# Biases of two adaLN gates placed in zeroed accumulators before the multiply-adds, and another background rate in the SwiGLU units

## The chip, the core and the metric

The kernel runs on one core of one Trainium2 chip (trn2). The metric is the device time of one execution in microseconds (us). Before the change three runs gave a median of 1597.8 us (1597.12 to 1598.16). Next to them stands one profiled execution with its trace; it took 1597.22 us, of which the profile's span covers 1595.4 us.

## What is computed

One layer of a decoder trunk for 256 tokens of width 2048, all in float32. Cut to what matters here:

```
mod = silu(c) @ w_ada + b_ada                      # 1 x 12288
shift1, scale1, gate1, shift2, scale2, gate2 = split(mod, 6)
h = rms_norm(x) * (1 + scale1) + shift1
x = x + gate1 * mixing_sublayer(h)                 # attention, dilated attention, GLA, w_out
h = rms_norm(x) * (1 + scale2) + shift2
x = x + gate2 * (silu(h @ w_gate) * (h @ w_up)) @ w_ffn_out
```

gate1 and gate2 are rows of 2048 numbers which multiply the columns of the outputs of the two halves. Each is one row vector times a 2048 x 2048 part of w_ada (16.8 MB), plus 2048 numbers of b_ada.

## The kernel before

**Main work.** All large products run on TensorE, in three matmuls for each pair of tiles: weights and activations are split into a high and a low part (`mm3`, lines 164 to 166). Weights come by SyncE's DMA queue (SP) in pieces of 128 x 1024 floats, 512 KB each, into four `raw` buffers (line 146, in the last stages line 1269). ScalarE casts a piece into `whi` (lines 158, 1276), VectorE subtracts to get `wlo` (lines 159, 1277), and there are four buffers of each. A piece feeds twelve matmuls of 512 columns in an ordinary block.

**Order.** The program is written for a tile framework. It works out the order of each engine's instructions ahead of time from priorities and readiness, and puts in the waits. Every engine, and the DMA queue of SP, then works strictly in that order. Loads are written inside `prio()`, which moves them 4000 places forward; a load then stands in the queue as soon as the framework believes that its buffer is free. `tc.issue_after(x)` keeps an instruction behind `x` on its engine.

**Background.** Four of the six parts of `mod` are worked out beside the main work. `ada_segment_steps` yields once for each of 32 loads of w_ada (128 rows x 1024 columns, line 375, into a ring of three or four buffers AR, KC, KD, OD). When the ring is full, `mac` puts the oldest piece's multiply-add on VectorE, behind the last weight split: acc += raw * silu(c) per row (`ada_mac`, line 288). The first piece of each half is a plain product which starts the accumulator (line 286). After the last multiply-add `done` is put into the list `after`. For the gates this is `rows_of`: four small loads of b_ada into a `scr` buffer (line 970) and four additions on row 0 of the accumulator (line 971), then four empty steps, and then for each of four quarters of 512 columns, twice: a cast on ScalarE (line 980), a subtraction on VectorE (line 981), and after two steps two matmuls with a matrix of ones (lines 985, 986), which sum over the 128 rows and spread the result. The quarter goes back to SBUF on ScalarE (line 987). That is 28 steps.

**Rate.** `tick(n)` adds n to a balance and does one step of the background list and one of `after` for each whole one in it. `block` ticks once for each two slices of 128 rows, with `state["rate"]`: RATE_MID 0.6 while gate1 is made, RATE_FFN 0.65 in the eleven units of the SwiGLU's first product, RATE_OUT 2.5 in the last product, where `fast_products` ticks with twice the rate, 5, for each entry of its order.

**Places.** gate1 uses the tiles T4 and T5. Their last readers before it are the matmuls of the GLA levels (lines 800 and 832). gate2 uses the tile `ada`, whose reader before it is the turning of the second normalised input (line 1192), early in unit 0. gate2's background is appended in unit 8; units 8, 9 and 10 are ordinary ones with two blocks of eight ticks each, so 48 ticks in all. Units 1 to 7 save an eighth of their products in the way of Strassen and have no background. After unit 10 comes `fast_products` with the order OUT_A: seven ordinary entries, then the fast ones in turn with ordinary ones. It calls `sums_of_unit` (lines 1432 to 1437, work for VectorE) at entries 1, 2 and 4, and `flush` at entry 7. gate2 is read behind that (line 1417).

Of the kernel before, what the change touches and what calls it, by code (L numbers as in the profile page):

```python
# [17 lines left out]
P = 128  # L18
T = 256
NT = T // P  # L20
D = 2048
KC = D // P
DFF = 5632
NB = 512
# [5 lines left out]
N_DIL = 6  # L30
N_GLA = 4
SEG_SHIFT1, SEG_SCALE1, SEG_GATE1, SEG_SHIFT2, SEG_SCALE2, SEG_GATE2 = range(6)
RATE_IN, RATE_MID, RATE_FFN = 0.8, 0.6, 0.65
RATE_OUT = 2.5
LOOK = 3
DEFER = 4
# [40 lines left out]
def trunk(ctx: ExitStack, tc: tile.TileContext, I, out):  # L77
    nc = tc.nc
# [10 lines left out]
    def nm(base):  # L89
        uid[0] += 1  # L90
        return f"{base}_{uid[0]}"

    def S(tag, shape, dtype=F32):
        return slot.tile(shape, dtype, tag=tag, name=nm(tag))
# [4 lines left out]
    def scr(shape, dtype=F32):  # L99
        return sp.tile(shape, dtype, tag="scr", name=nm("scr"))  # L100
# [4 lines left out]
    def misc_bank(shape):  # L105
        return psm.tile(shape, F32, tag="misc", name=nm("misc"))

    @contextmanager
    def prio(offset=AHEAD):

        with tc.high_priority(offset=offset):
            start = tc.cur_priority
            yield
            n = tc.cur_priority - start
        tc.cur_priority += n
# [164 lines left out]

    w_ada = I["w_ada"]

    def ada_mac(acc, raw, k):
        c = csil[:, k : k + 1]
        if k == 0:
            nc.vector.tensor_scalar(acc, raw, c, None, op0=ALU.mult)
        else:
            nc.vector.scalar_tensor_tensor(acc, raw, c, acc, op0=ALU.mult, op1=ALU.add)  # L288
# [5 lines left out]
    def ada_group(k0, k1, tags=ADA_TAGS, between=None):  # L294
# [5 lines left out]
        for i in range(pieces):  # L300
            a = k0 + n * i // pieces
            m = k0 + n * (i + 1) // pieces - a
            w = m * P
            acc = S("ada", [P, 2, w])
            for k in range(KC):
                with prio():
                    raw = S(tags[count % len(tags)], [P, 2, w])
                    nc.sync.dma_start(
                        raw,
                        w_ada[k * P : (k + 1) * P, : 2 * D].rearrange("p (s c) -> p s c", s=2)[:, :, a * P : a * P + w],  # L310
                    )
                    with tc.issue_after(state["macs_after"]) if "macs_after" in state else nullcontext():
                        ada_mac(acc, raw, k)
                count += 1
                if k < KC - 1:
                    yield
            if between is not None:
                between()
            with prio():
                c = slice(a - k0, a - k0 + m)  # L320
                sums = small([P, 2, m])
                for j in range(2):
                    turned_sums(sums[:, j, :], acc[:, j, :])
                finish_columns(sums[:, 0, :], sh[:, c], SEG_SHIFT1, a)
                finish_columns(sums[:, 1, :], sc[:, c], SEG_SCALE1, a, ROW_N1)
            yield
# [25 lines left out]
    def araw(shape, dtype=F32):  # L352
        ring["n"] += 1
        return S(ring["tags"][ring["n"] % len(ring["tags"])], shape, dtype)

    macs = []

    def mac():
        acc, j, k, raw, done = macs.pop(0)
        with tc.issue_after(state["split"].ins):  # L360
            ada_mac(acc[j], raw, k)
        if done is not None:
            after.append(done)

    def ada_segment_steps(acc, seg, done):


        for k in range(KC):
            for j in range(2):
                while len(macs) >= len(ring["tags"]):  # L370
                    mac()
                raw = araw([P, 2 * NB])
                c0 = seg * D + j * 2 * NB
                with prio():
                    nc.sync.dma_start(raw, w_ada[k * P : (k + 1) * P, c0 : c0 + 2 * NB])
                macs.append((acc, j, k, raw, done if (k, j) == (KC - 1, 1) else None))
                yield

    def last_macs():
        while macs:  # L380
            mac()
            yield
# [121 lines left out]
    def first_group():  # L504
# [28 lines left out]
        for k in range(KC - 1):  # L533
            with tc.issue_after(split.ins) if k > 3 else nullcontext():
                ada_mac(acc, raws[k], k)
# [42 lines left out]
    for g in range(len(GROUPS) - 1):  # L578
        nxt = ada_group(*GROUPS[g + 1])
        steps = KC * -(-(GROUPS[g + 1][1] - GROUPS[g + 1][0]) // 4)  # L580
        done = 0
# [373 lines left out]
    def columns(seg, acc):  # L955
        for _ in range(4):
            yield
        v = const.tile([P, KC], F32, name=nm("mod2"))
        for i in range(0, KC, 4):
            turned_sums(v[:, i : i + 4], acc[:, i * P : (i + 4) * P], state["mm"].ins)  # L960
            yield
        finish_columns(v, v, seg, 0, ROW_N2 if seg == SEG_SCALE2 else None)
        mod2[seg] = v

    def rows_of(name, seg, acc):

        quarters = [a[:, c : c + NB] for a in acc for c in (0, NB)]
        for j, q in enumerate(quarters):
            br = scr([1, NB])
            nc.sync.dma_start(br, I["b_ada"][:, seg * D + j * NB : seg * D + (j + 1) * NB])  # L970
            nc.vector.tensor_add(q[0:1, :], q[0:1, :], br)
            yield
        for _ in range(4):
            yield
        for q in quarters:
            ps = misc_bank([P, NB])
            for c in (slice(0, T), slice(T, NB)):
                hl = S("T6", [P, 2, T], F32R)
                hi, lo = hl[:, 0, :], hl[:, 1, :]
                nc.scalar.copy(hi, q[:, c])  # L980
                nc.vector.tensor_tensor(lo, q[:, c], hi.bitcast(F32), op=ALU.subtract)
                yield
                yield
                with tc.issue_after(state["mm"].ins):
                    nc.tensor.matmul(ps[:, c], ones_r, hi, start=True, stop=False)
                    nc.tensor.matmul(ps[:, c], ones_r, lo, start=False, stop=True)
            nc.scalar.copy(q, ps)
            yield
        state[name] = quarters

    def halves(acc):
        return [acc[:, : 2 * NB], acc[:, 2 * NB :]]

    def background():
        for seg in (SEG_SHIFT2, SEG_GATE1, SEG_SCALE2):
            if seg == SEG_GATE1:
                acc = [S(f"T{4 + j}", [P, 2 * NB]) for j in range(2)]
                yield from ada_segment_steps(acc, seg, rows_of("gate1", seg, acc))
            else:
                acc = S("ada", [P, D])  # L1000
                yield from ada_segment_steps(halves(acc), seg, columns(seg, acc))
        yield from last_macs()

    bg.append(background())
    for b in range(0, 3):
        proj_block(LAST, b)
# [155 lines left out]
    gate1 = state["gate1"]  # L1162
# [75 lines left out]
    w_ff = I["w_ffn_in"]  # L1238

    def gate2_bg():  # L1240
        acc = halves(S("ada", [P, D]))
        yield from ada_segment_steps(acc, SEG_GATE2, rows_of("gate2", SEG_GATE2, acc))
        yield from last_macs()

    def sums_of(sf, h, a, b):
# [122 lines left out]
    for i in range(NFF):  # L1368
# [4 lines left out]
        if i == FAST[-1] + 1:  # L1373
            bg.append(gate2_bg())
# [71 lines left out]
    gate2 = state["gate2"]  # L1446
# [55 lines left out]
```

## Time and profile before

| what | value |
|---|---|
| median of three runs | 1597.8 us (1597.12 to 1598.16) |
| profiled execution | 1597.22 us |
| its span | 1595.4 us, 20167 instructions |
| TensorE (PE) busy | 1582.0 us, 99% |
| weight loads of TensorE (PEld) busy | 1308.2 us, 82% |
| VectorE (DVE) busy | 1275.5 us, 80% |
| ScalarE (ACT) busy | 837.6 us, 53% |
| GpSimd (POOL) busy | 5.3 us in 14 instructions |
| DMA | 395.97 MB, mean 248 GB/s |

Busy time of an engine is the time in which at least one of its instructions runs. A matmul's record (0.39 us for 512 columns) is longer than the distance from one matmul to the next, since they are pipelined; a short wait can lie hidden in it. Times in the views are us from the start of the span. In a view of waits a row says who waited for whom, the total, how many times, and the longest.

### The profile page before, as it was taken

The numbers are of one execution on the slowest core, as the hardware profiler recorded it, in microseconds if no ns is written. First come the engines' busy times: TensorE is split into PE (matmuls) and PEld (weight loads), VectorE is DVE, ScalarE is ACT, GpSimd is POOL, SyncE is SP. The second block draws the span as 40 slices with busy tenths as digits, with TensorE's granted clock in tenths as the row PEclk, the third lists the DMA queues.
The fourth block names the chain that finished last, engine by engine and source line by source line (L and its number), as shares of the span: only waits on it lengthen the run. The fifth ranks groups of instructions, "written<-read, shape, count | busy, mean of one in ns | idle before, by whom it ended". The sixth has DMA issues, their size and how long they took to land.

```text
span 1595.4 us, 20167 instructions
## 1 busy us (share of the span) xinstructions
PE 1582.0 (99%) x7272; PEld 1308.2 (82%) x7272; DVE 1275.5 (80%) x1523; ACT 837.6 (53%) x1184; POOL 5.3 (0%) x14
## 2 busy tenths in 40 slices
PE   8999999999999999999999999999999999999998
PEld 7878888888888888888887888888888888778887
DVE  6889995888878787878756688888887677988884
ACT  5654449775754434444446655555454443554552
POOL 1000000000000000000000000000000000000000
PEclk9999999999999999999999999999999999999999
DMA  9999997667778889989766466556657889667664
GB/s 339 365 326 320 332 302 245 214 189 257 247 258 280 297 301 314 311 289 310 228 192 210 149 196 195 192 184 193 205 183 226 281 302 314 203 196 225 212 204 140
DMA packets 194596, 395.97 MB, mean 248 GB/s; under 512 B 12914, under 2 KB 27928, under 8 KB 194496
## 3 DMA queue, kind: packets, MB, share of 16 engines
q1 hardware_dynamic: 194096, 394.60, 75.0%
q8 instruction: 57, 0.93, 0.2%
q14 instruction: 43, 0.35, 0.1%
q10 hardware_dynamic: 176, 0.07, 0.0%
q0 software_dynamic: 224, 0.01, 0.0%
HBM read 392.53 MB, written 2.10 MB: 247 GB/s over the span
## 4 chain that ended last, share of the span: by engine, by line
PE 85%; DMA 5%; DVE 5%; ACT 3%; issue 2%; SPq 0%; ACTq 0%; DVEq 0%
PE acc L166 21%; PE acc L165 21%; PE acc L164 20%; PE misc L164 6%; PE misc L166 6%; PE misc L165 6%; DVE wlo L159 1%; ACT whi L158 1%; DMA AR<-w_ada 1%; DVE ada L288 1%; DMA raw<-w_br_gla 1%; DMA raw<-w_ffn_out 1%; PE acc L434 1%; DMA raw<-w_in 1%; PE misc L800 1%
## 5 line engine op out<-in xcount | busy, mean ns | idle before, releaser
L158 ACT CAST whi<-raw 128x1024 fp32r<-128x1024 f32 x362 | 368.6, 1022 | 412.2 <-PE acc L166 264.9
L159 DVE TENSOR_TENSOR wlo<-raw,whi 128x1024 fp32r<-128x1024 f32 x362 | 425.6, 1183 | 186.0 <-ACT whi L158 184.4
L164 PE MATMUL acc<-whi,H 128*128 128x512 f32 x1308 | 511.9, 392 | 1.2 <-ACT H L446 0.8
L165 PE MATMUL acc<-wlo,H 128*128 128x512 f32 x1308 | 510.9, 391 | 0.8 <-DVE wlo L159 0.7
L166 PE MATMUL acc<-whi,H 128*128 128x512 f32 x1308 | 509.8, 390 | 0.4 <-DVE H L453 0.4
L166 PEld LDWEIGHTS acc<-whi,H 128*128 128x128 f32 x1308 | 245.3, 188 | 52.9 <-DVE H L453 1.6
L164 PEld LDWEIGHTS acc<-whi,H 128*128 128x128 f32 x1308 | 245.5, 188 | 52.3 <-ACT H L446 1.3
L165 PEld LDWEIGHTS acc<-wlo,H 128*128 128x128 f32 x1308 | 245.7, 188 | 51.3 <-DVE wlo L159 1.7
L1276 ACT CAST whi<-raw 128x1024 fp32r<-128x1024 f32 (+1 forms) x184 | 179.2, 992 | 134.5 <-PE acc L166 68.0
L1277 DVE TENSOR_TENSOR wlo<-raw,whi 128x1024 fp32r<-128x1024 f32 (+1 forms) x184 | 205.2, 1145 | 19.8 <-ACT whi L1276 18.8
L164 PE MATMUL misc<-whi,H 128*128 128x512 f32 x246 | 96.1, 391 | 0.0
L165 PE MATMUL misc<-wlo,H 128*128 128x512 f32 x246 | 95.8, 389 | 0.0
L166 PE MATMUL misc<-whi,H 128*128 128x512 f32 x246 | 95.8, 389 | 0.0
L164 PE MATMUL acc<-whi,A 128*128 128x512 f32 x222 | 87.1, 394 | 0.5 <-ACT whi L1276 0.4
L165 PE MATMUL acc<-wlo,A 128*128 128x512 f32 x222 | 86.7, 390 | 0.8 <-DVE wlo L159 0.8
L166 PE MATMUL acc<-whi,A 128*128 128x512 f32 x216 | 84.3, 390 | 0.0
L288 DVE SCALAR_TENSOR_TENSOR ada<-AR,csil,ada 128x1024 f32<-128x1024 f32 x59 | 74.8, 1278 | 3.6 <-DMA AR<-w_ada 3.6
L165 PEld LDWEIGHTS misc<-wlo,H 128*128 128x128 f32 x246 | 46.2, 188 | 9.7 <-DVE wlo L1277 0.2
L166 PEld LDWEIGHTS misc<-whi,H 128*128 128x128 f32 x246 | 46.2, 188 | 9.5
L164 PEld LDWEIGHTS misc<-whi,H 128*128 128x128 f32 x246 | 46.2, 188 | 9.5
L164 PEld LDWEIGHTS acc<-whi,A 128*128 128x128 f32 x222 | 41.7, 188 | 9.6 <-ACT whi L1276 1.1
L165 PEld LDWEIGHTS acc<-wlo,A 128*128 128x128 f32 x222 | 41.7, 188 | 9.6 <-DVE wlo L159 1.1
(428 smaller groups left out, 1927.6 us busy)
## 6 DMA issues: line engine op xcount, KB each, us to landing
raw<-w_in SPq DMA_DIRECT2D x205, 512.0 KB, 4.8
raw<-w_ffn_in SPq DMA_DIRECT2D x176, 512.0 KB, 4.2
raw<-w_ffn_out SPq DMA_DIRECT2D x88, 512.0 KB, 4.8
AR<-w_ada SPq DMA_DIRECT2D x79, 512.0 KB, 5.1
raw<-w_out SPq DMA_DIRECT2D x32, 512.0 KB, 4.8
KC<-w_ada SPq DMA_DIRECT2D x30, 512.0 KB, 6.2
OS<-w_ada SPq DMA_DIRECT2D x16, 512.0 KB, 6.9
KD<-w_ada SPq DMA_DIRECT2D x16, 512.0 KB, 5.8
```

The lines of the kernel that those rows point to most:

```text
L158: state["cast"] = nc.scalar.copy(hi[:, :n, :], raw[:, :n, :])
L159: state["split"] = nc.vector.tensor_tensor(lo[:, :n, :], raw[:, :n, :], hi[:, :n, :].bitcast(F32), op=ALU.subtract)
L164: nc.tensor.matmul(ps, lh, rh, start=start, stop=False, skip_group_check=seeded)
L165: nc.tensor.matmul(ps, lh, rl, start=False, stop=False, skip_group_check=seeded)
L166: state["mm"] = nc.tensor.matmul(ps, ll, rh, start=False, stop=stop, skip_group_check=seeded)
L288: nc.vector.scalar_tensor_tensor(acc, raw, c, acc, op0=ALU.mult, op1=ALU.add)
L434: state["warm"] = nc.tensor.matmul(ps, ones_r, wide, start=True, stop=True)
L800: nc.tensor.matmul(ps[:n, t * N_GLA + h, :].rearrange("p (s l) -> p s l", l=L), at(f, h, t)[:, :n], odd(at(f, h, t)), start=True, stop=True,)
L1276: nc.scalar.copy(hi[:, :n, :], src)
L1277: state["split"] = nc.vector.tensor_tensor(lo[:, :n, :], src, hi[:, :n, :].bitcast(F32), op=ALU.subtract)
```

## The change

The addition of the bias after the sum is replaced: the accumulators of the two gates are set to zero by GpSimd, b_ada is loaded into their first row by one DMA for each half, inside `prio()`, and the first multiply-add then adds as the others do. The four load-and-add steps of `rows_of` go. RATE_FFN becomes 0.75.

```diff
-RATE_IN, RATE_MID, RATE_FFN = 0.8, 0.6, 0.65
+RATE_IN, RATE_MID, RATE_FFN = 0.8, 0.6, 0.75
...
-    def ada_mac(acc, raw, k):
+    def ada_mac(acc, raw, k, zero=True):
+
         c = csil[:, k : k + 1]
-        if k == 0:
+        if k == 0 and zero:
             nc.vector.tensor_scalar(acc, raw, c, None, op0=ALU.mult)
         else:
             nc.vector.scalar_tensor_tensor(acc, raw, c, acc, op0=ALU.mult, op1=ALU.add)
...
+    def biased(acc, seg):
+
+        for j, a in enumerate(acc):
+            nc.gpsimd.memset(a, 0.0)
+            with prio():
+                nc.sync.dma_start(a[0:1, :], I["b_ada"][:, seg * D + j * 2 * NB : seg * D + (j + 1) * 2 * NB])
+        return acc
...
     def rows_of(name, seg, acc):
 
         quarters = [a[:, c : c + NB] for a in acc for c in (0, NB)]
-        for j, q in enumerate(quarters):
-            br = scr([1, NB])
-            nc.sync.dma_start(br, I["b_ada"][:, seg * D + j * NB : seg * D + (j + 1) * NB])
-            nc.vector.tensor_add(q[0:1, :], q[0:1, :], br)
-            yield
...
-                acc = [S(f"T{4 + j}", [P, 2 * NB]) for j in range(2)]
-                yield from ada_segment_steps(acc, seg, rows_of("gate1", seg, acc))
+                acc = biased([S(f"T{4 + j}", [P, 2 * NB]) for j in range(2)], seg)
+                yield from ada_segment_steps(acc, seg, rows_of("gate1", seg, acc), False)
...
-        acc = halves(S("ada", [P, D]))
-        yield from ada_segment_steps(acc, SEG_GATE2, rows_of("gate2", SEG_GATE2, acc))
+        acc = biased(halves(S("ada", [P, D])), SEG_GATE2)
+        yield from ada_segment_steps(acc, SEG_GATE2, rows_of("gate2", SEG_GATE2, acc), False)
         yield from last_macs()
```

`zero` is carried along through `ada_segment_steps` and the list `macs` to `ada_mac`.

More of the change, by code (lines that the diff above doesn't have):

```diff
@@ L358, in mac, with ada_segment_steps @@
     def mac():
-        acc, j, k, raw, done = macs.pop(0)
+        acc, j, k, raw, done, zero = macs.pop(0)
         with tc.issue_after(state["split"].ins):
-            ada_mac(acc[j], raw, k)
+            ada_mac(acc[j], raw, k, zero)
         if done is not None:
             after.append(done)
-    def ada_segment_steps(acc, seg, done):
+    def biased(acc, seg):
[4 more added lines that the diff above has]
+        return acc
+    def ada_segment_steps(acc, seg, done, zero=True):
         for k in range(KC):
@@ L375, in ada_segment_steps @@
                     nc.sync.dma_start(raw, w_ada[k * P : (k + 1) * P, c0 : c0 + 2 * NB])
-                macs.append((acc, j, k, raw, done if (k, j) == (KC - 1, 1) else None))
+                macs.append((acc, j, k, raw, done if (k, j) == (KC - 1, 1) else None, zero))
                 yield
```

## The prediction

> **What bounds the kernel now.** I read the table of busy time first, then the waits of TensorE over the whole span, and then windows around the two gates.
>
> ```profile
> PE 1582.0 (99%) x7272; PEld 1308.2 (82%) x7272; DVE 1275.5 (80%) x1523; ACT 837.6 (53%) x1184; POOL 5.3 (0%) x14
> ```
> ```profile
> engine line waited for: us in total, times, longest us
> PE misc L216 <- DMA H<-c: 2.4, 1, 2.4
> PE acc L165 <- DVE wlo L159: 1.4, 2, 0.8
> PE misc L985 <- ACT T L980: 0.8, 1, 0.8
> ...
> PE acc L164 <- ACT whi L1276: 0.4, 1, 0.4
> ```
>
> TensorE is the bound: 1582.0 of 1595.4 us. No row of its waits is over 2.4 us, and the change adds and removes no matmul. So it can gain only where TensorE stands still near the gates, and lose only by a new stop. The windows show where that is. gate1's sums and rows lie in 440 to 740. The end of the units I find by the turning of unit 10's result, which stands at entry 1 of the last product:
>
> ```profile
> 1358.33 1.04 PE L1115 MATMUL misc<-ident,scr 128*128 128x128 f32 x8
> ```
>
> One entry is 24 matmuls at 0.23 us (the distance is shown below), 5.5 us; so entry 0 starts near 1353, and units 8 to 10, 48 pieces of twelve matmuls, 132.5 us, start near 1220. gate2's rows lie in 1370 to 1403.
>
> ```profile
> core 0: us, PE busy (x) PEld busy (x) DVE busy (x) ACT busy (x) POOL busy (x), PEclk, DMA share, GB/s
> 440.00:480.00 40.00, 39.83 (x198) 33.36 (x197) 30.61 (x47) 20.47 (x27) 0.00 (x0) 1.00 0.77 254
> ...
> 540.00:620.00 80.00, 79.24 (x354) 65.21 (x353) 64.21 (x64) 33.47 (x36) 0.00 (x0) 1.00 0.88 293
> 620.00:740.00 120.00, 120.00 (x542) 99.72 (x541) 94.05 (x91) 55.63 (x66) 0.00 (x0) 1.00 0.90 306
> ...
> 1270.00:1315.00 45.00, 45.00 (x206) 37.42 (x205) 34.53 (x32) 19.36 (x21) 0.00 (x0) 1.00 0.88 302
> 1315.00:1360.00 45.00, 45.00 (x204) 37.34 (x203) 35.63 (x33) 18.55 (x21) 0.00 (x0) 1.00 0.92 317
> 1360.00:1380.00 20.00, 19.18 (x85) 15.34 (x83) 19.09 (x23) 8.48 (x11) 0.00 (x0) 1.00 0.79 253
> 1380.00:1410.00 30.00, 29.20 (x128) 22.57 (x128) 27.76 (x40) 18.43 (x26) 0.00 (x0) 1.00 0.46 140
> ```
>
> In the units TensorE never stops (45.00 of 45.00), with VectorE at 79% and the DMA at 0.92 of its time in the last one. Where gate2's rows are made it stops for 0.82 and 0.80 us, and there VectorE is nearly full (19.09 of 20). The timeline of TensorE shows the stops one by one.
>
> ```profile
> 1371.26 0.39 PE L166 MATMUL acc<-whi,A 128*128 128x512 f32 x1
> 1371.49 0.39 PE L164 MATMUL acc<-whi,A 128*128 128x512 f32 x1
> 1372.70 0.39 PE L985 MATMUL misc<-T,ones_r 128*128 128x256 f32 x1 [0.82 <-ACT T L980]
> ...
> 1379.75 0.39 PE L165 MATMUL acc<-wlo,A 128*128 128x512 f32 x1
> 1380.29 0.38 PE L986 MATMUL misc<-T,ones_r 128*128 128x256 f32 x1
> ...
> 1398.88 0.39 PE L166 MATMUL misc<-whi,H 128*128 128x512 f32 x1
> 1399.30 0.38 PE L985 MATMUL misc<-T,ones_r 128*128 128x256 f32 x1
> 1399.76 0.39 PE L986 MATMUL misc<-T,ones_r 128*128 128x256 f32 x1
> 1400.24 0.50 PE L164 MATMUL acc<-whi,A 128*128 128x512 f32 x1
> 1401.19 0.51 PE L164 MATMUL acc<-whi,A 128*128 128x512 f32 x1 [0.45 <-ACT whi L1276]
> ```
>
> The usual distance is 0.23 us (1371.26 to 1371.49), so a stop is the distance less 0.23. That gives 0.98 at 1372.70 and 0.31 at 1380.29, both before a matmul of gate2's rows. The last four distances are 0.42, 0.46, 0.48 and 0.95, so 0.19, 0.23, 0.25 and 0.72, together 1.39. In all 2.68 us. The fifth stop near the gates is at 573, where a weight split is late:
>
> ```profile
> 571.81 0.50 PE L164 MATMUL acc<-whi,A 128*128 128x512 f32 x1
> 573.07 0.50 PE L165 MATMUL acc<-wlo,A 128*128 128x512 f32 x1 [0.76 <-DVE wlo L159]
> ```
>
> It costs 1.26 less 0.23, 1.03 us. With 2.68 that is 3.7 us: the most that this change can win.
>
> **The change part by part.** *VectorE's instructions.* Medians by line, and the groups of 1358 to 1403:
>
> ```profile
> L286 DVE TENSOR_SCALAR ada<-AR,csil x4: 748/748/749, 273.9 to 1233.8; 128x1024 f32<-128x1024 f32 x4
> ...
> L288 DVE SCALAR_TENSOR_TENSOR ada<-KC,csil,ada x20: 1275/1279/1286, 400.5 to 1369.2; 128x1024 f32<-128x1024 f32 x20
> ...
> L971 DVE TENSOR_TENSOR T<-T,scr x4: 671/673/680, 602.2 to 621.0; 1x512 f32<-1x512 f32 x4
> L971 DVE TENSOR_TENSOR ada<-ada,scr x4: 672/673/675, 1371.5 to 1377.4; 1x512 f32<-1x512 f32 x4
> ```
> ```profile
> L971 DVE TENSOR_TENSOR ada<-ada,scr 1x512 f32<-1x512 f32 x4 | 2.6, 673 | 0.0
> L288 DVE SCALAR_TENSOR_TENSOR ada<-KC,csil,ada 128x1024 f32<-128x1024 f32 x2 | 2.6, 1280 | 0.2 <-DMA KC<-w_ada 0.2
> L288 DVE SCALAR_TENSOR_TENSOR ada<-AR,csil,ada 128x1024 f32<-128x1024 f32 x2 | 2.6, 1278 | 0.0
> ```
>
> Eight additions go, 8 x 0.673 = 5.4 us. Four first products become multiply-adds, 4 x (1.278 - 0.748) = 2.1 us more; gate2's are near 1234 in unit 8, where TensorE does not stop. Neither is a gain by itself; VectorE is not the bound outside 1360 to 1403.
>
> *The rate.* 48 ticks at 0.65 make 31.2 steps, so before, the last load and the last multiply-adds fall into the next stage (four of them, 2.6 + 2.6 us, after 1358). At 0.75 they make 36: 32 loads, the three last multiply-adds, and the first step or two of `rows_of`. The last multiply-add then comes at tick 35 / 0.75 = 46.7 of 48, some 4 us before 1353 instead of at 1369. `rows_of` has 24 steps instead of 28. At 5 steps for each entry it ends near entry 4 instead of entry 6, two entries of 24 matmuls at 0.23 us earlier: 11 us. So between 1358 and 1403 VectorE loses the additions (2.6) and the four multiply-adds (5.2): 7.8 of some 43 us. It was at 95% there; it would be near 78%, as in the units.
>
> *What that gives.* The stops of 1399 to 1401, 1.39 us, come where the last quarter's casts and splits meet the first fast entry. With the rows 11 us earlier and VectorE with room, I take all of it away. The first two stops, 1.29 us, are of another kind: the matmul of a row stands in TensorE's queue ahead of a cast or a split that has still to be done. The order stays as it was written, only earlier, so I leave them.
>
> *Zeroing.* The trace has no such memset on GpSimd. The nearest rows:
>
> ```profile
> 0.73 0.20 POOL masks.py:197 MEMSET ident<- 128x128 f32 x1 [0.29 <-POOLq L1487]
> ...
> 245.92 1.04 POOL L605 CAST KC<-T 128x1024 uint8<-128x1024 f32 x1 [240.92 <-DMA T<-k_lvl]
> ```
>
> By the first, a half of 128 x 1024 takes at most 8 x 0.20 = 1.6 us, by the second about 1.0; I take 1.0, the row with the same shape. GpSimd does nothing else after 247, so it starts when the tile's last reader is through:
>
> ```profile
> L832 PE MATMUL misc<-T x8: 270/275/275, 377.4 to 378.2; 128*128 128x128 f32 x8
> ...
> L1192 PE MATMUL misc<-ident,ada x32: 272/273/329, 866.8 to 883.7; 128*128 128x128 f32 x32
> ```
>
> That is near 379 for gate1 (T5) and near 884 for gate2, the latter 350 us before its first product at 1233.8. Their time is hidden unless they hold up somebody else. VectorE's fast form of one-input work is visible above (0.748 us for the shape that takes the multiply-add 1.278). [...]
>
> *The bias DMAs.* Eight small loads leave SP's queue and four come in. One of the old ones held the queue up:
>
> ```profile
> SPq L970 <- PE misc L938: 6.3, 1, 6.3
> ```
>
> That was inside the window of 440 to 480, where TensorE stopped for 0.17 us in all (39.83 of 40): loads run far enough ahead to cover 6.3 us. The new ones may hold it up too, since each waits for its memset at a place fixed ahead of time, with weight loads behind it, then the casts, splits and matmuls that need them. Bounds: nothing, or a wait as long as that one, which costs nothing either; a gain by the hold that goes is at most the 0.17. I take 0. Gate1's place (379) has the busier queue; at 884 the DMA has time.
>
> *More loads in the units.* 48 weight loads of 0.524 MB in 132.5 us are 190 GB/s; gate2 at 0.65 adds 123, at 0.75 it adds 142. So 332 instead of 313 GB/s while it lasts. The windows of the units reached 317 at a share of 0.92, and earlier the queue has carried more:
>
> ```profile
> 60.00:80.00 20.00, 20.00 (x90) 16.54 (x89) 16.65 (x17) 11.86 (x18) 0.00 (x0) 1.00 1.04 380
> ```
>
> I take 0 here; the other end is 332 / 317 - 1 = 4.7% of the 118 us that 32 steps last, 5.6 us.
>
> **Sum.** 1597.22 - 1.39 = 1595.8 us for an execution like the profiled one. The median stands 0.6 us above it, so the forecast is 1597.8 - 1.4 = **1596.4 us**.
>
> **Rivals.** (1) *The stops only move.* Rows made beside entries 0 to 4 meet `sums_of_unit` at entries 1, 2 and 4 as before, and a cast is late at another place. The rate changes when work is queued, not what paces it: 1597.8 us. For it: two of the stops are of that kind. Against it: VectorE's 7.8 us.
> (2) *All near stops go*, that at 573 too, by the other order of the queue: 1597.8 - 3.7 = 1594.1 us. Against it: nothing moves at 573 itself, where a load of w_br_gla comes late.
> (3) *DMA in units 8 to 10 becomes the bound.* If this mixture of loads holds no more than the 317 GB/s of its best window, the weights fall 5.6 us behind and the gain of 1.4 is all that stands against it: 1597.8 + 5.6 - 1.4 = 1602.0 us. It decides from a ceiling below 332 GB/s. Against it: 380 GB/s at 60 to 80, and no stop at 317.
> (4) *SP stands before a bias load.* If the queue reaches it twice as early as the old one, the wait is 12.6 us, of which 6.3 are shown to be covered: 1604.1 us. For it: waits of 6.3 us do happen. Against it: it must be double.
> [...]
>
> **Chances.** Forecast 0.52; (1) 0.22; (2) 0.08; (3) 0.11; (4) 0.05; (5) 0.02. A measurement of this kernel can tell about 0.2%, 3.2 us, from no change: faster is below 1594.6, slower above 1601.0. Faster is (2), 0.08. Slower is (4), most of (3) and half of (5): 0.05 + 0.08 + 0.01 = 0.14. The rest, 0.78, is the same. The range goes from (2) to (3), 1594.1 to 1602.0 us.
>
> **What would show it.** Right: no line 971; memsets of about 1 us near 379 and 884; the last multiply-add of gate2 before 1353 and its last row matmul near 1390, not 1400; VectorE below 85% and fewer stops in 1380 to 1410. Wrong: TensorE waiting for `wlo` or `whi` in 1220 to 1353 with the DMA share near 1 (3); a wait of SP for a memset of over 6 us, and TensorE stopped behind it (4); VectorE idle beside a memset (5); the same 2.7 us of stops elsewhere (1).

## The result, and the profile after

The changed kernel takes 1606.79 us (median of six runs, 1603.95 to 1609.65), the kernel before, on the same chip, 1598.49 us (six runs, 1597.12 to 1599.81). The ratio is 1.0051 with a 95% interval of 1.0037 to 1.0065: about 8 us slower, outside the predicted range. The profiled execution after took 1608.22 us with a span of 1606.4 us, 11.0 us more than the span before.

The table of busy time of the kernel after, and TensorE's waits over its whole span (who waited for whom, total, times, longest):

```profile
PE 1585.8 (99%) x7272; PEld 1310.9 (82%) x7272; DVE 1274.2 (79%) x1515; ACT 837.8 (52%) x1184; POOL 9.1 (1%) x18
```
```profile
PE misc L989 <- ACT T L984: 4.6, 1, 4.6
PE misc L216 <- DMA H<-c: 2.5, 1, 2.5
PE acc L165 <- DVE wlo L1281: 2.2, 2, 2.0
PE acc L165 <- DVE wlo L159: 1.4, 2, 0.8
```

Two rows are new, of 4.6 and 2.2 us. From here on lines are those of the kernel after: multiply-add L289, load of w_ada L384, row cast and matmuls L984, L989 and L990, loads and splits of the last stages L1273 and L1281, the up-multiply of a unit (the product that empties the accumulators of its second block) L1403; before they were L288, L375, L980, L985 and L986, L1269 and L1277, L1399.

Windows of the kernel after; the first is also shown of the kernel before, in a fence of its own:

```profile
core 0: us, PE busy (x) PEld busy (x) DVE busy (x) ACT busy (x) POOL busy (x), PEclk, DMA share, GB/s
1220.00:1340.00 120.00, 120.00 (x543) 99.42 (x542) 90.87 (x86) 50.40 (x54) 0.00 (x0) 1.00 0.84 284
1340.00:1350.00 10.00, 8.80 (x38) 6.72 (x37) 4.86 (x5) 3.54 (x4) 0.00 (x0) 1.00 0.96 326
1350.00:1360.00 10.00, 5.39 (x24) 4.19 (x24) 8.67 (x8) 3.65 (x5) 0.00 (x0) 0.87 0.90 298
1360.00:1370.00 10.00, 10.00 (x39) 7.94 (x39) 8.64 (x13) 3.77 (x6) 0.00 (x0) 0.79 0.51 169
1380.00:1410.00 30.00, 29.81 (x133) 23.91 (x132) 23.06 (x30) 15.56 (x19) 0.00 (x0) 1.00 0.45 145
1420.00:1430.00 10.00, 8.56 (x31) 6.91 (x32) 7.67 (x10) 2.27 (x4) 0.00 (x0) 0.83 0.60 190
```
```profile
1220.00:1340.00 120.00, 120.00 (x543) 99.58 (x543) 87.27 (x83) 51.32 (x55) 0.00 (x0) 1.00 0.84 280
```

Up to 1340 nothing shows: TensorE never stops, and the DMA moves 284 GB/s, hardly more than before. Then TensorE loses time on both sides of the end of the units, and again in 1420 to 1430. The row of 1360 to 1370 needs a second look. TensorE is busy for 10.00 of 10.00 us, but with 39 matmuls, where 45 are usual in ten us (543 in the 120 of the first row): the granted clock is 0.79. The timeline of TensorE shows both losses:

```profile
1354.35 0.39 PE L165 MATMUL acc<-wlo,H 128*128 128x512 f32 x1
1354.58 0.39 PE L166 MATMUL acc<-whi,H 128*128 128x512 f32 x1
1359.58 0.58 PE L989 MATMUL misc<-T,ones_r 128*128 128x256 f32 x1 [4.61 <-ACT T L984]
1359.95 0.63 PE L164 MATMUL acc<-whi,A 128*128 128x512 f32 x1
1360.38 0.63 PE L165 MATMUL acc<-wlo,A 128*128 128x512 f32 x1
...
1363.80 0.56 PE L164 MATMUL acc<-whi,A 128*128 128x512 f32 x1
1364.20 0.39 PE L165 MATMUL acc<-wlo,A 128*128 128x512 f32 x1
1364.43 0.39 PE L166 MATMUL acc<-whi,A 128*128 128x512 f32 x1
```

The first matmul of gate2's rows comes 5.00 us after the one ahead of it, 4.77 more than the usual 0.23. Behind it the distance is 0.43 from 1359.95 to 1364.20, ten matmuls at about half speed, 2.0 us; then it is 0.23 again.

**The account.** By distances less 0.23, the kernel after loses 0.60 and 1.03 us near 1345, 4.77 at the first row matmul, 2.0 by the low clock, 2.19 at 1419 (a split of w_ffn_out is late), about 1.5 by a second stretch of low clock at 1422 to 1426, and 0.55, 0.35 and 0.98 at other places (709, 1408, 1472): 14.0 us. Of the 3.7 us of stops that the prediction counted in the kernel before none is left at its old place. 14.0 - 3.7 = 10.3 of the 11.0 us.

Why is the first row matmul late? ScalarE and VectorE of the kernel after, from one view of each:

```profile
1344.38 1.05 ACT L158 CAST whi<-raw 128x1024 fp32r<-128x1024 f32 x1 [4.94 <-DMA raw<-w_ffn_in]
...
1359.12 0.41 ACT L984 CAST T<-ada 128x256 fp32r<-128x256 f32 x1 [4.06 <-DVE ada L289]
```
```profile
1357.80 1.28 DVE L289 SCALAR_TENSOR_TENSOR ada<-AR,csil,ada 128x1024 f32<-128x1024 f32 x1 [1.33 <-DMA AR<-w_ada]
1359.00 1.22 DVE L1281 TENSOR_TENSOR wlo<-raw,whi 128x1024 fp32r<-128x1024 f32 x1
1360.13 1.28 DVE L1403 TENSOR_TENSOR scr<-scr,acc 128x512 f32<-128x512 f32 x2
1361.33 1.28 DVE L289 SCALAR_TENSOR_TENSOR ada<-KC,csil,ada 128x1024 f32<-128x1024 f32 x1
```

The row matmul waits for its cast, the cast for the last multiply-add of its half, and that one for a load of w_ada. The last multiply-add of all ends at 1362.6, not before 1353. And near 1344 ScalarE had stood for 4.94 us for a weight load. Both loads stand in SP's queue; its order in the kernel after:

```profile
1334.84 0.33 SPq L384 DMA_DIRECT2D AR<-w_ada  x1
1337.17 0.33 SPq L384 DMA_DIRECT2D KC<-w_ada  x1
1337.92 0.89 SPq L146 DMA_DIRECT2D raw<-w_ffn_in  x2
1340.70 0.34 SPq L384 DMA_DIRECT2D AR<-w_ada  x1
...
1341.83 9.18 SPq L1273 DMA_DIRECT2D raw<-w_ffn_out  x4
1351.84 0.34 SPq L384 DMA_DIRECT2D AR<-w_ada  x1
1353.03 0.34 SPq L384 DMA_DIRECT2D KC<-w_ada  x1
```
```profile
SPq L384 <- DVE ada L289: 7.1, 4, 2.0
SPq L384 <- DMA AR<-w_ada: 1.1, 1, 1.1
SPq L1273 <- DVE wlo L159: 0.2, 1, 0.2
```

The second fence is what SP's queue waited for in 1330 to 1343: 7.1 of 13 us for multiply-adds that free the ring's buffers, and only 0.2 for a buffer of the weights. So the two weight loads of 1337.92 were ready and only stood behind gate2's; the cast of the first is the one of 1344.38. Further on it is the other way about: gate2's last two loads, 1351.84 and 1353.03, stand behind four loads of w_ffn_out.

### The profile page after: what moved, and what is told of

The parts are those of the page before. It is cut to its first block, busy times and chain, and to the rows that moved or that the text cites. A ratio compares the mean times of both kernels' runs of the same rounds, so it can differ in the third digit from the quotient of the medians.

```text
span 1606.4 us, 20180 instructions
## 1 busy us (share of the span) xinstructions
PE 1585.8 (99%) x7272; PEld 1310.9 (82%) x7272; DVE 1274.2 (79%) x1515; ACT 837.8 (52%) x1184; POOL 9.1 (1%) x18
## 4 chain that ended last, share of the span: by engine, by line
PE 82%; DMA 8%; DVE 5%; ACT 3%; issue 2%; SPq 0%; DVEq 0%; ACTq 0%
PE acc L166 20%; PE acc L165 20%; PE acc L164 20%; PE misc L166 6%; PE misc L165 6%; PE misc L164 6%; DMA raw<-w_ffn_out 2%; DMA raw<-w_in 1%; DMA AR<-w_ada 1%; DMA raw<-w_ffn_in 1%; DVE wlo L159 1%; DVE ada L289 1%; DVE wlo L1281 1%; ACT whi L158 1%; DMA OS<-w_ada 1%
## 5 line engine op out<-in xcount | busy, mean ns | idle before, releaser
L1281 DVE TENSOR_TENSOR wlo<-raw,whi 128x1024 fp32r<-128x1024 f32 (+1 forms) x184 | 205.1, 1146 | 20.5 <-ACT whi L1280 19.2
L289 DVE SCALAR_TENSOR_TENSOR ada<-AR,csil,ada 128x1024 f32<-128x1024 f32 x60 | 76.5, 1282 | 6.6 <-DMA AR<-w_ada 6.6
L1280 ACT CAST whi<-AR 128x1024 fp32r<-128x1024 f32 x24 | 25.3, 1053 | 49.3 <-PE acc L166 24.3
```

The source lines that it names most:

```text
L1280: nc.scalar.copy(hi[:, :n, :], src)
L1281: state["split"] = nc.vector.tensor_tensor(lo[:, :n, :], src, hi[:, :n, :].bitcast(F32), op=ALU.subtract)
```

## The experiments

Three theories were tried, the second in two forms. **T1**: the rows come too early, so that TensorE meets the first row matmul before its last multiply-add; placed later, they would cost nothing. **T2**: the loads of gate2, at the new rate, make the weights and the multiply-adds late at the end of the units, either by their bytes (**T2a**) or by their place in SP's queue (**T2b**). **T3**: the zeroing and the bias DMAs.

### One part of the change at a time

The changed kernel with the old rate:

```diff
-RATE_IN, RATE_MID, RATE_FFN = 0.8, 0.6, 0.75
+RATE_IN, RATE_MID, RATE_FFN = 0.8, 0.6, 0.65
```

> The changed kernel with RATE_FFN back at 0.65: the bias part alone. Theory T1 (rows too early): in TensorE's queue gate2's first row matmul stands 23 places ahead of where it stands before the change (81 in the changed kernel), so it is reached near 1366.5, while its last multiply-add ends near 1368: a stop of 1 to 2 us in place of the old one of 1.0, in all 0 to 3 us over the kernel before. T2 (the units' extra loads make weights late): as before the change, within 1 us. T3 (zeroing and bias DMAs cost): all of the 8 us stay.

Measured: 1598.86 us, ratio 1.0003 (0.9995 to 1.0012). (Each ratio is to runs of the kernel before on the same chip.) The kernel before with the new rate alone:

```diff
-RATE_IN, RATE_MID, RATE_FFN = 0.8, 0.6, 0.65
+RATE_IN, RATE_MID, RATE_FFN = 0.8, 0.6, 0.75
```

> The kernel before with RATE_FFN at 0.75: the rate alone. T1: the first row matmul stands 50 places ahead of the old place, reached near 1360 to 1362, and its multiply-adds end near 1359: no stop over 1 us there, within 2 us of the kernel before. T2: 1.6 us of late weights near 1344 and the late ones of the last product stay, 5 to 8 us slower. T3: as before the change.

Measured: 1603.25 us, 1.0029 (1.0019 to 1.0039), 4.7 us slower. T2 comes nearest: its late weights near 1344 are there (stops of 1.28 and 1.03 us), the time is just short of its 5 to 8 us. T1 fails: a stop of 1.74 us stands at the first row matmul, and the time is more than 2 us off. The bias of gate1 alone done in the new way, gate2 and the rate as before (the four additions for gate2 come back with it):

```diff
...
-        acc = biased(halves(S("ada", [P, D])), SEG_GATE2)
-        yield from ada_segment_steps(acc, SEG_GATE2, rows_of("gate2", SEG_GATE2, acc), False)
+        acc = halves(S("ada", [P, D]))
+        yield from ada_segment_steps(acc, SEG_GATE2, rows_of("gate2", SEG_GATE2, acc))
```

> The kernel before with the new bias for gate1 alone (memset, bias DMA, no additions), gate2 and the rate as before. T1 and T2: within 1 us of the kernel before. T3: about half of the loss, 3 to 5 us slower.

Measured: 1599.75 us, 1.0007 (0.9998 to 1.0017). And the changed kernel with a rate of 0.70:

```diff
-RATE_IN, RATE_MID, RATE_FFN = 0.8, 0.6, 0.75
+RATE_IN, RATE_MID, RATE_FFN = 0.8, 0.6, 0.70
```

> The changed kernel with RATE_FFN 0.70: weights and gate2 together 323 GB/s instead of 332 (0.75) and 313 (0.65). T2a with a ceiling near the 317 GB/s of the best window before: about half of the loss, 3 to 5 us over the kernel before. T2b: the order changes by steps, anything from 0 to 6 us, and the stops stand where weight loads wait behind gate2's.

Measured: 1598.24 us, 0.9997 (0.9988 to 1.0006). The 3 to 5 us of T2a do not come. T2b allowed 0 to 6 us, too wide to be tested by this, and the stops are not where it had them: 1.99 us at the first matmul of the next stage and 1.42 at the first row matmul.

T3 falls: at the old rate the new way of the bias costs nothing that can be measured, for one gate or for both. The rate carries the loss, and not in proportion: with the new bias 0.05 more is free, 0.10 more costs 8 us. The rate alone costs 4.7 of these 8 us. At the new rate the bias part is not free, 1.0051 against 1.0029 (the intervals just touch). The traces point to the first row matmul, which comes earlier with four steps fewer: its stop is 4.77 us, against 1.74.

### The rows later

The changed kernel with fourteen empty steps, not four, ahead of gate2's rows:

```diff
-        for _ in range(4):
+        for _ in range(14 if name == "gate2" else 4):
```

> The changed kernel with fourteen empty steps instead of four ahead of gate2's rows, nothing else: first row matmul 31 places ahead of the old place, reached near 1365, five us behind its multiply-adds. T1: the stop of 4.6 us and the slow clock behind it are gone, 6 to 8 us faster than the changed kernel, within 2 us of the kernel before. T2 and T3: stays 8 us slower than before.

Measured: 1604.75 us, 1.0035 (1.0023 to 1.0048). About two of the eight us come back, not all (five runs, and the interval overlaps that of the changed kernel). The 4.6 us at the row matmul are gone, and TensorE's waits of this kernel in 1340 to 1430 have another row in their place; VectorE's timeline says why:

```profile
PE acc L164 <- DVE scr L1403: 3.1, 1, 3.1
PE acc L165 <- DVE wlo L1281: 1.5, 1, 1.5
```
```profile
1360.01 1.29 DVE L289 SCALAR_TENSOR_TENSOR ada<-AR,csil,ada 128x1024 f32<-128x1024 f32 x1 [1.04 <-DMA AR<-w_ada]
1361.22 1.22 DVE L1281 TENSOR_TENSOR wlo<-raw,whi 128x1024 fp32r<-128x1024 f32 x1
1362.35 1.28 DVE L1403 TENSOR_TENSOR scr<-scr,acc 128x512 f32<-128x512 f32 x2
```

The up-multiply frees accumulators that TensorE needs at the start of the next stage. On VectorE it stands behind the same multiply-add that waits for the same late load. So T1 names one of two things that the late load stops, not the cause. The same edit at the old rate (twelve empty steps, the changed kernel otherwise):

> The bias part with RATE_FFN 0.65, and twelve empty steps instead of four ahead of gate2's rows: the first row matmul stands 7 places ahead of its old place instead of 23, behind the end of its multiply-adds. Both theories: the stop of 1.1 us at the first row matmul of the bias part alone goes, and VectorE keeps the room of the additions that went: 0 to 2 us faster than the kernel before.

Measured: 1597.04 us, 0.9997 (0.9988 to 1.0005). The stop at the first row matmul is gone, but in the profiled execution 1.76 us stand at a later row matmul and 1.55 at the first matmul behind the units: the stops moved.

### The bytes, the ring, the order of the loads

*Half the bytes.* gate2's loads bring 512 of their 1024 columns and each multiply-add reads them twice, so that its work on VectorE is the same (gate2's second and fourth quarters are left out: they repeat the first and the third):

```diff
...
+                w = NB if seg == SEG_GATE2 else 2 * NB
                 with prio():
-                    nc.sync.dma_start(raw, w_ada[k * P : (k + 1) * P, c0 : c0 + 2 * NB])
+                    nc.sync.dma_start(raw[:, :w], w_ada[k * P : (k + 1) * P, c0 : c0 + w])
+                if w == NB:
+                    raw = raw[:, :w].unsqueeze(1).to_broadcast([P, 2, NB])
```

> The changed kernel in which gate2's loads bring only the first 512 of each 1024 columns and the multiply-add reads these twice: half of gate2's bytes, the same instructions, buffers and queue order (gate2's second and fourth quarter are not computed). The rate is the cause now; T1 has fallen. Theory T2a (bytes): at 0.75 weights and gate2 together want more than the DMA brings, loads land late. Expected: stops of 1344 to 1365 gone, the time within 3 us of the kernel before. Theory T2b (order): weight loads stand in SP's queue behind gate2's loads that wait for a ring buffer, which a multiply-add frees on VectorE's pace whatever the bytes. Expected: the same stops, still 5 us or more over the kernel before.

Measured: 1598.1 us, 0.9998 (0.9989 to 1.0007). The loss is gone, with the rate and the multiply-adds as in the changed kernel. So it is the loads, and not VectorE's work: T2. This is what T2a expected, and the stops that T2b expected did not come. But the smaller loads also hold SP's queue for less time (24.5 us in 1220 to 1360, against 40.8 in the changed kernel, a view that is shown below), so a and b stay open.

*A smaller ring* in the kernel before, old rate:

```diff
-    ring["tags"] = ("AR0", "AR1", "KC")
+    ring["tags"] = ("AR0", "AR1")
```

> The kernel before with two ring buffers instead of three in the units, rate 0.65: the same bytes, but each of gate2's loads waits for a later multiply-add and holds SP's queue longer. T2a: within 1.5 us of the kernel before. T2b: stops in the units, 4 us or more slower.

Measured: 1601.89 us, 1.002 (1.0011 to 1.0029). Neither form had this. With two buffers the first row matmul stops for 3.3 us, with five matmuls at half speed behind it (granted clock 0.91 in the mean of 1360 to 1380), so 3.6 us are lost without the new rate. But TensorE does not stop in the units, and the weights are as early as in the kernel before (the table of leads below): here only the multiply-adds and what hangs on them are late (the last starts at 1370.9, before at 1369.2).

*The order of the loads.* The changed kernel, rate 0.75, with gate2's loads outside `prio()`, so that they take their place in SP's queue in the order in which they are written:

```diff
-                with prio():
+                with prio() if seg != SEG_GATE2 else nullcontext():
```

> The changed kernel, rate 0.75, with gate2's loads outside prio(), nothing else: the same bytes at the same rate, but in SP's queue they now stand one by one between weight loads, where in the changed kernel weight loads come in bunches of four behind gate2's. T2a (bytes alone): weights land late as before, stops near 1344 stay, 5 us or more over the kernel before. T2b (bytes and bunches together): no late weights near 1344; the stop at gate2's first row matmul, which stands in the same place, may stay by up to 4 us: 0 to 4 us over the kernel before.

Measured: 1599.72 us, 1.0012 (1.0003 to 1.0021). With the fourteen empty steps as well:

> The same with fourteen empty steps ahead of gate2's rows, as in the changed kernel with later rows (which was 6 us over the kernel before). T2a: no better than that one. T2b: neither late weights nor a stop at the first row matmul: within 2 us of the kernel before, or under it.

Measured: 1598.01 us, 1.0002 (0.9993 to 1.0011). Same bytes, same rate, same multiply-adds, and three quarters of the loss are gone, with the later rows all of it. Both are as T2b had it; the late weights that T2a expected near 1344 did not come. The windows of the kernel with the new order alone:

```profile
1220.00:1340.00 120.00, 120.00 (x543) 99.58 (x543) 94.25 (x89) 51.52 (x55) 0.00 (x0) 1.00 0.86 299
1340.00:1350.00 10.00, 10.00 (x46) 8.29 (x45) 7.07 (x6) 4.16 (x4) 0.00 (x0) 1.00 0.91 320
```

The DMA moves more than in the changed kernel (299 against 284 GB/s) and TensorE does not stop. T2a, a ceiling of the DMA, falls. What SP's queue waited for in 1220 to 1360, one row each, of the kernel before, of the changed one, and of this one:

```profile
SPq L375 <- DVE ada L288: 38.1, 26, 2.6
```
```profile
SPq L384 <- DVE ada L289: 40.8, 29, 2.6
```
```profile
SPq L384 <- DVE ada L289: 7.7, 10, 0.8
```

Of 140 us the queue stands for 38 to 41 behind a load of gate2 that has no free buffer; in the new order for 7.7. But the first row is as long as the second, and the kernel before loses nothing by it: the length of the hold does not tell the kernels apart. How early the weights are does. The lead in this table is the time from the end of a piece's split on VectorE to the second of its twelve matmuls, the first that reads `wlo`, in the mean of the last eight pieces of unit 10; the hold is the row of SP's queue above.

| kernel | ratio | hold, us | lead, us |
|---|---|---|---|
| before | 1 | 38.1 | 5.0 |
| new bias, 0.65 | 1.0003 | 39.8 | 4.8 |
| new bias, 0.70 | 0.9997 | 39.7 | 3.4 |
| rate 0.75 alone | 1.0029 | 38.4 | 1.1 |
| as changed, 0.75 | 1.0051 | 40.8 | 0.9 |
| as changed, loads in turn | 1.0012 | 7.7 | 5.1 |
| as changed, half the bytes | 0.9998 | 24.5 | 5.6 |
| before, two ring buffers | 1.0020 | 32.4 | 5.1 |

In the changed kernel the lead is 4.7, 3.3 and 0.9 us in the last three groups of eight pieces, in the kernel before 4.6, 5.4 and 5.0. So at 0.75 the lead of the weights is used up by the end of the units, and a smaller rate, half the bytes or loads in turn each keep it. It takes the bytes and the place in the queue together. Why the lead goes only over the last sixteen pieces is not shown.

*The old rate with the new order*, without and with twelve empty steps; the two edits are those shown:

> The bias part at rate 0.65 with gate2's loads outside prio(). A candidate to beat both kernels. T2a: as the bias part alone, within 1 us of the kernel before. T2b: the stops of 0.8 and 1.1 us where the units end get shorter: 0 to 3 us faster than the kernel before.

Measured: 1597.47 us, 0.9992 (0.9983 to 1.0001). That is 1.0 us under the kernel before and not clear of noise, so it does not decide between the two. The stop of 0.8 us is gone; the one at the first row matmul is 1.50 us, longer and not shorter.

> The changed kernel with the old rate 0.65, gate2's loads outside prio(), and 12 empty steps instead of 4 ahead of gate2's rows. The same without the later rows had 1.50 us of stop at its first row matmul (1369.4), 0.41 near 1462 and 0.35 near 573. Theory (loads in turn keep the weights early; the first row matmul only has to come behind its last multiply-add): the stop at the first row matmul goes and nothing comes in its place before 1400; median 1596.0 to 1597.0 us, a ratio of 0.998 to 0.999 to the kernel before. Rival (a stop behind the units only moves): another stop of 1 to 2 us near 1375 to 1415, median 1597.5 to 1598.5 us, ratio 0.999 to 1.000.

Measured: 1596.8 us, 0.999 (0.9981 to 0.9999), a span of 1593.4 us. It is the one version whose interval stays below 1, though only just (0.9999); among thirteen versions one such interval can be chance. The profiled execution, at 1595.2 us, is one of its fastest. Behind the units, where the kernel before stopped for 2.7 us, it hardly stops at all:

```profile
1360.00:1410.00 50.00, 49.99 (x225) 39.98 (x224) 47.26 (x62) 29.34 (x39) 0.00 (x0) 1.00 0.63 215
```

### All eight beside each other

The bias part in all of them; ratio to the kernel before:

| gate2's loads | rows | rate 0.65 | rate 0.75 |
|---|---|---|---|
| ahead (in `prio()`) | as changed | 1.0003 | 1.0051 |
| ahead | later | 0.9997 | 1.0035 |
| in turn | as changed | 0.9992 | 1.0012 |
| in turn | later | 0.9990 | 1.0002 |

The rate costs 0.48 and 0.38% where the loads stand ahead, 0.20 and 0.12% where they stand in turn (differences along the rows; with intervals of about 0.1% on each ratio the last is not clear of noise). Part of what is left at 0.75 in turn is the first row matmul again: in the new order it still stops for 1.25 us at 1354.

How late the up-multiply is also goes with the rate and the order of the loads. Its start in the profiled execution, counted from the last turning of the second normalised input (883.7 in the kernel before and after):

| kernel | L1403 starts after | TensorE's stop for it, us |
|---|---|---|
| before | 470.6 | none |
| in turn, 0.75, rows later | 470.5 | none |
| in turn, 0.65 | 470.9 | none (1.50 at the row matmul) |
| in turn, 0.75 | 471.0 | none (1.25 at the row matmul) |
| in turn, 0.65, rows later | 471.4 | 0.37 |
| ahead, 0.65 | 471.9 | 0.79 |
| ahead, 0.65, rows later | 472.6 | 1.55 |
| ahead, 0.70 | 473.0 | 1.99 |
| ahead, 0.75, rows later | 474.4 | 3.22 |
| ahead, 0.75, the rate alone | 476.2 | 2.70 |
| ahead, 0.75, as changed | 476.4 | the row matmul stops first, 4.77 |

From some 471 us on TensorE waits, and most of each us more is paid. The rate alone stops for less than its 476.2 suggest because TensorE had already lost 2.3 us near 1345.

**What stays open.** The stop near 1411 to 1420, with a low clock behind it in some versions (0.83 in 1420 to 1430 of the changed kernel, 0.91 in 1410 to 1430 with the rate alone, 1.00 there with half the bytes), is in every kernel at 0.75, with half the bytes too (1.79 us), and in none at 0.65 or 0.70. VectorE's timeline of the changed kernel suggests that its splits for the first fast entries fall into one bunch, so that four loads of w_ffn_out leave late:

```profile
1407.64 4.09 DVE L1281 TENSOR_TENSOR wlo<-raw,whi 128x1024 fp32r<-128x1024 f32 x4
...
1419.56 0.69 DVE L1284 TENSOR_TENSOR AR<-raw,raw 128x512 f32<-128x512 f32 x1 [2.75 <-DMA raw<-w_ffn_out]
```

No run isolates that. The six runs of the changed kernel spread over 5.7 us, those of the kernel before over 2.7; that tells nothing, since 25 runs of the kernel before spread over 5.8. One stop that differs from execution to execution stands near 415, long before the units: 0.32 us in the profile of the kernel before, 2.12 in that of gate1 alone, 2.74 with a low clock behind it in that of the later rows at 0.75 (mean clock of that execution 0.997).

## Why the prediction was wrong, point by point

**Zeroing: right.** The timeline of GpSimd after:

```profile
372.25 0.95 POOL L369 MEMSET T<- 128x1024 f32 x1 [125.74 <-PE misc L809]
378.81 0.95 POOL L369 MEMSET T<- 128x1024 f32 x1 [5.60 <-DMA AR<-w_ada]
884.06 1.85 POOL L369 MEMSET ada<- 128x1024 f32 x2 [504.30 <-PE misc L1196]
```

0.95 us each, where the sum had 1.0, at 372, 379 and 884, about as said. Taking the cast of the same shape for the price, and not eight times the small memset, was the better choice. **The bias DMAs: right.** One row of SP's waits over the whole span answers rival (4), 4.0 us and not over 6:

```profile
SPq L371 <- POOL ada L369: 4.0, 2, 3.4
```

No run shows the blocking of VectorE by a memset for which (5) stands in the chances, with 0.02, and with 0.01 in the 0.14 for slower: TensorE is busy for 20.00 of 20.00 us in 365 to 385, before and after, VectorE's split and multiply-add beside the memset of 378.81 take 1.22 and 1.28 us, as elsewhere, and the runs at the old rate (1.0003 and 1.0007, upper ends 1.0012 and 1.0017) bound any cost of the memsets below 0.2%.

**VectorE's relief: half of it came, and it was worth nothing that can be measured.** Between 1358 and 1403, where "near 78%" was forecast, VectorE goes from 41.77 to 38.07 of 45.00 us, 93 to 85%: 3.7 us less, not 7.8. Two of the four multiply-adds that were to go still run there. In 1380 to 1410 it falls from 27.76 of 30 to 23.06, 77%, as the signs of being right had it, TensorE's stops there go from 0.80 to 0.19 us, and the last row matmul is at 1387 where 1390 was forecast. The stops of 1399 to 1401 are gone, with the bias part alone too; but in that kernel 0.79, 1.09 and 0.62 us of stops stand at 1357, 1368 and 574 instead. Rival (1), that stops only move, describes the bias part (1.0003): the gain of 1.39 us did not come even without the new rate.

**"The last multiply-add then comes ... some 4 us before 1353": wrong, by 12 us.** The step counted ticks and took the step's place in the program for the time of its work. In the kernel before, VectorE already ran behind its ticks: a multiply-add needs its load, that one a free buffer, and that one an earlier multiply-add. The row that would have shown it stands in the prediction: the kernel before starts its last multiply-add at 1369.2. With 31.2 steps done at 1353 and five for each entry of 5.5 us, its step, the 35th, was due near 1357; it ran 12 us late. The kernel after starts it at 1361.3 where 1349 was due: late by the same 12 us. The prediction put this lateness at nothing.

**"The order stays as it was written, only earlier, so I leave them": wrong, and it follows from that.** TensorE reaches the first row matmul 16.9 us earlier than before (0.23 behind the matmul ahead of it: 1371.7 before, 1354.8 after). What it needs comes only 13.1 us earlier: before, the addition of the bias, which ended at 1372.2, now its half's last multiply-add, which ends at 1359.1. The difference, 3.8 us, is what the stop grew by, from 0.98 to 4.77.

**"More loads in the units ... I take 0": wrong, and the larger error.** The other end of that term, 5.6 us, and rival (3), 1602.0, were the nearest in kind to what came, and (3)'s mark is there: TensorE waits for `whi` and `wlo` near 1345 at a share of 0.96. (Rival (4) gave a nearer time, 1604.1, but SP never stood 6 us before a bias load.) But its mechanism is not the one at work. No ceiling at 317 GB/s was met: the changed kernel moves 326 in 1340 to 1350, and the same loads in another order moved at 299 in the mean and cost a quarter. The prediction weighed mean GB/s, 313 against 332 by its sum, where the traces have 280 and 284, and did not ask which load stands behind which in SP's queue. It quoted one wait of SP at gate1 and did not read those of the units, where 38 us of hold already stood. What the term should have held is the lead of the weights, which falls from 5.0 to 0.9 us.

**Not foreseen:** behind two stops of TensorE, of 4.77 and 2.19 us, its matmuls ran at half clock, which cost 2.0 and about 1.5 us more, some 3.5 of the 11.0 us of the profiled execution.

## What to carry to other kernels

Before a background is made faster, read what the queue that carries its loads waits for: if loads that wait for a buffer of the background stand ahead of the main work's, a higher rate can use up the lead of the main work's loads though the mean bandwidth hardly changes (here 5.0 us became 0.9, at 280 and 284 GB/s). Measure that lead, not the length of the wait. Ask of every step that is placed earlier whether the last thing it needs comes earlier by as much; a place in the program is not a time. And when a wait is moved away, look for the next instruction that stands behind the same late one: here it was the up-multiply, for which the very next matmul in TensorE's queue waited.

## What the runs showed of the hardware

**TensorE's clock stood at half around some of its stops.** The window of 1361 to 1363 of the changed kernel shows half the clock, that of 1365 to 1367 the full one:

```profile
1361.00:1363.00 2.00, 2.00 (x7) 1.52 (x6) 2.00 (x3) 0.00 (x0) 0.00 (x0) 0.50 0.74 232
1365.00:1367.00 2.00, 2.00 (x11) 1.67 (x10) 1.23 (x2) 1.36 (x2) 0.00 (x0) 1.00 0.76 255
```

In the changed kernel the clock stands at 0.5 for 6.8 us around the stop of 4.77, from 1357.3 to 1364.2, and for 3.4 us behind the stop of 2.19, from 1422.2 to 1425.6. In the other versions the mean clock of a window shows it: 0.91 in 1360 to 1380 with the stop of 3.33 us (two ring buffers) and with that of 3.22 (later rows at 0.75), 0.91 in 1410 to 1430 with that of 2.49 (the rate alone), 0.67 in 1415 to 1420 with that of 2.11 (loads in turn at 0.75). Around other stops it does not fall: 1.00 in 1360 to 1380 with the stop of 2.70 us (the rate alone) and with that of 1.99 (0.70), and 1.00 in the mean of the execution with that of 2.12 (gate1 alone). So the length of the stop does not decide alone: 2.11 us had half clock behind it, 2.70 had not. Two executions at 0.65, with later rows and with loads in turn, have a mean clock of 0.999, and their longest stops behind the units are 1.76 and 1.50 us. What decides is not shown.
